# Gated delta net projections: queries and keys handed on before values, convolution taps read from PSUM, weights in blocks of one feature tile

## The chip, the cores and the metric

The kernel runs on one core of a Trainium2 chip. The metric is device time in microseconds (us) of one execution, lower is better. Before the change the median of 3 runs is 1668.59 us (1667.01 to 1671.13). The engines are named as the profile names them: PE (TensorE; PEld is its weight load), DVE (VectorE), ACT (ScalarE), POOL (GpSimd) and SP, whose queue issues the weight transfers.

## The reference

Two transformer blocks one after the other, in float32, on 272 tokens (16 meta tokens and 256 of the input) of width 1024; 48 rows of padding at the front are masked in the reference. The change is in one mixer only, the gated delta net of the first layer. Cut to that:

```python
proj = h @ w_in                        # 272 x 1024 @ 1024 x 6176
qkv = silu(causal_depthwise_conv(proj[..., :4096], conv_w))    # 4 taps per feature
z = proj[..., 4096:6144]               # output gate; two more groups give beta and g
q, k, v = split(qkv)                   # 8 heads of 128 for q and k, 16 for v
q, k = l2_normalize(q), l2_normalize(k)
# per chunk and head: A = I + tril(k k^T * beta * decay); solve A X = [v*beta, k*beta*exp(G)]
# scan over chunks: v_new = u - w S;  o = q S + attn v_new;  S = S*gt + k^T v_new
out = (rms_norm(o) * silu(z)) @ w_out
```

Everything else of the two blocks (residual additions, the feed-forward blocks, an mLSTM, three attention branches) is unchanged.

## The kernel before

Activations lie feature by feature: a tile holds 128 features on the partitions and 272 tokens along the free axis. A float32 product is made of three float32r matmuls, high by high, high by low and low by high. `wload` (L357) brings a block of weights of 512 KB from HBM into one of 3 `wraw` buffers; ACT rounds it to the high part `wh` (CAST), and POOL, in this stage, subtracts to get the low part `wl` in two halves. `linear_g` (L398) then accumulates, for one or two tiles of 128 output features, 24 matmuls of 272 columns per tile into the PSUM tiles `ps`, of which there are two, and calls a function on each finished tile.

In this stage that function is `conv4` (L974). ACT copies the PSUM tile to `cx` in SBUF and scales it by the last tap into `cy`; DVE adds the three other taps from `cx`; ACT takes a tanh (`cth`), and DVE or, for features from tile 14 on, POOL, makes the activated tile `kv`. `gdn_proj` (L991) does so for a group g of the four groups of heads: two tiles of keys, two of queries, four of values, each pair from blocks of 256 columns and 4 of the 8 input tiles, that is two blocks per pair.

A chain then follows for each group and each of two chunks c of 128 tokens. `before` (L1349) waits until all of `gdn_proj` is done. `unit_kq` (L1003) transposes queries and keys (`kqp`), sums squares on ACT, takes an inverse root in 11 small DVE operations (`rq_v`, `rq_y`, `rq_a`), scales (`kqtok`) and transposes back. `gdn_pre` (L1118) makes the decays (`dp`, ACT exponential `BA`), the products `kk`, and the token-major values (`vp`, `bv`). `gdn_core` (L1145) inverts the triangular matrix in doubling steps (`rtp` first, then `yp`, `Y`, `w` and the update of `RT` on DVE, at the end `zp`, `r2p`), applies it (`up`) and advances the state (`sp`, `op`); four lanes, each with its own PSUM bank, take the four groups one after the other. `after` (L1366) normalises and transposes back (`otp`). A short tail handles the last 16 tokens. `gdn_gates` (L899) makes beta and the decays' exponents from a narrow product `psba`: about twenty DVE operations on `lp`, `gg`, sums `gp` on PE, and `stk`, `rp`, `rw`.

The order on PE is written while the program is recorded. Each piece of work is a generator that yields what it will need; `Threads.run` (L153) takes the first live generator, in the list's order, whose inputs a small model of the engines holds to be ready. The chains stand ahead of the projections in that list, so the projections' matmuls (in steps of three) fill PE where no chain step counts as ready. PE then runs this order as written and waits at any instruction whose input is late. The order on DVE, ACT and POOL is made by the scheduler of the language below. The last piece of projection work is `gdn_z` (L1440), eight pairs of gate tiles; after it `project_out` starts with the matmuls `ps<-og`.

Of the kernel before, what the change touches and what calls it, by code (L numbers as in the profile page):

```python
# [21 lines left out]
T = S + NM  # L22
# [186 lines left out]
class Kern:  # L209
    def __init__(self, ctx, tc, ins, out):  # L210
        self.tc, self.nc, self.ctx = tc, tc.nc, ctx
        nc = tc.nc
        self.th = Threads()
        self.mem_done, self.half = Event(), Event()
        self.pause = [Event() for _ in range(3)]
        self.mwt = {}
        self.ready = {}
        self.V, self.A, self.PE, self.G = (self.th.engine(*e) for e in (
            ("V", nc.vector), ("A", nc.scalar), ("PE", nc.tensor), ("G", nc.gpsimd)))
        self.SY = nc.sync  # L220
        self.i = ins
        self.out = out

        self.const = self.pool(ctx, "const", 1)
        self.p_raw = self.pool(ctx, "praw", 3)
        self.p_hl = self.pool(ctx, "phl", 3)
        self.p_x = self.pool(ctx, "px", 8)
        self.p_h = self.pool(ctx, "ph", 14)
        self.p_s = self.pool(ctx, "psm", 2)
        self.p_t = self.pool(ctx, "ptiny", 2)  # L230
        self.lane = None
        self.ordered = False
        self.mixing = False
        self.near_load = self.seg = 0
        self.mid = None
        self.gctx = ExitStack()
        self.pp = self.pool(self.gctx, "pq", 2, space=PSUM)
        self.p_v = self.pool(self.gctx, "pkvg", 8)
        self.p_l = self.pool(self.gctx, "plane", 1)
        self.p_lp = self.pool(self.gctx, "planep", 1, space=PSUM)  # L240
# [37 lines left out]
        return t  # L278

    def ps(self, shape=(128, T), name="ps"):  # L280
        return self.pp.tile(list(shape), F32, tag="pp", name=name)

    def pcore(self, shape=(128, 4, 128), name="pcs"):
        return self.pc.tile(list(shape), F32, tag="pc", name=name)
# [533 lines left out]
    def embed(self):  # L818
# [15 lines left out]
        with self.tc.manual_schedule(engines={mybir.EngineType.DVE}):  # L834
# [21 lines left out]
            for t, (o, P) in enumerate(TT):  # L856
                self.ts(rd[:P, t, :P], self.ident[:P, :P], r[:P, t:t + 1], ALU.mult)
            self.columns(self.norms, 0)
            low = {1: prefetch(0, KD, 6144, 32), 3: prefetch(0, 4, 1024, 256), 6: prefetch(4, 4, 1024, 256)}
            self.masks()  # L860
            for k in range(KD):
                self.lane = k % 4
# [11 lines left out]
    def residual(self):  # L874

        for k in range(KD):
            yield [f"p{k % 4}", 10.0 + 1.0 * k]
            self.lane = k % 4
            p = self.plane("trx", (128, T))
            for t, (o, P) in enumerate(TT):  # L880
                self.tr(p[:, o:o + P], self.xt[t][k // 4][:P, (k % 4) * 128:(k % 4) * 128 + 128], P)
            self.A.copy(self.hs[k], p[:])
# [91 lines left out]
    def conv4(self, ps, ct, out):  # L974

        w = lambda j: self.pv(PV_GC + j * 32 + ct)
        y = self.sm(name="cy")
        x = self.p_l.tile([128, T], F32, tag="cx", name="cx", bufs=3)
        self.A.copy(x[:], ps)
        self.act(y[:], ps, AF.Copy, scale=w(3))  # L980
        for s in (1, 2, 3):
            self.stt(y[:, s:], x[:, :T - s], w(3 - s), y[:, s:], ALU.mult, ALU.add)
        th = self.sm(name="cth", tag="th")
        self.act(th[:], y[:], AF.Tanh, scale=0.5)
        if ct >= 14:
            self.tt(th[:], th[:], y[:], ALU.mult, self.G)
            self.tt(out, th[:], y[:], ALU.add, self.G)
        else:
            self.stt(out, th[:], 1.0, y[:], ALU.add, ALU.mult)

    def gdn_proj(self, X, g):  # L991
        W = self.i["gdn_w_in"][0]
        qs, ks, v0, v1 = (self.vslot() for _ in range(4))
        for base, dst in ((1024 + g * 256, ks), (g * 256, qs), (2048 + g * 512, v0), (2304 + g * 512, v1)):
            yield from self.linear_g(W, base, 256, KD, X, T, lambda m, p: self.conv4(p, base // 128 + m, dst[:, m, :]))
        tl = slice(256, T)
        self.G.tensor_copy(self.kqtail[:, 0, 2 * g:2 * g + 2, :], ks[:, :, tl])
        self.G.tensor_copy(self.kqtail[:, 1, 2 * g:2 * g + 2, :], qs[:, :, tl])
        for n, v in enumerate((v0, v1)):
            self.G.tensor_copy(self.vtail[:, 4 * g + 2 * n:4 * g + 2 * n + 2, :], v[:, :, tl])  # L1000
        return qs, ks, (v0, v1)

    def unit_kq(self, x, c):  # L1003


        n = len(x)
        yield list(x) + [f"pu{c}"]
        self.lane = f"u{c}"
        ss = self.tiny([128, n], "kqss")
        p = self.plane("kqp", (128, n, 128))  # L1010
        for h in range(n):
# [6 lines left out]
        kq = self.ring(f"kq{c}", "kqtok", (128, n, 128))  # L1018
        for h in range(n):
            self.act(kq[:, h, :], p[:, h, :], AF.Copy, scale=r[:, h:h + 1])  # L1020
        yield [kq[:], f"pu{c}", 0.8]
        self.lane = f"u{c}"
        p2 = self.plane("kqp2", (128, n, 128))
        for h in range(n):
            self.tr(p2[:, h, :], kq[:, h, :])
# [89 lines left out]
        self.tt(e[:], kk[:, :, None, :].to_broadcast([128, 2, 2, 128]), e[:], ALU.mult)  # L1115
        return e

    def gdn_pre(self, q, c, kqT, v):  # L1118


        sl = slice(c * 128, c * 128 + 128)
        h0 = 2 * q
# [9 lines left out]
                    self.mm(d[:, kind, h, :], selc(kind, h), rw, kind == 0 and h == 0, False)  # L1132

        BA = yield from self.decays(kqT[:, 0, :], kqT, diff, 0, self.nG[:, c, h0:h0 + 2])
        yield [BA[:], f"pu{c}"]
        self.lane = f"u{c}"
        vp = self.plane("vp")
        bv = self.ring(f"bv{c}", "bv")
# [1 line left out]
            self.tr(vp[:, h, :], v[:, h, sl])  # L1140
        for h in range(2):
            self.act(bv[:, h, :], vp[:, h, :], AF.Copy, scale=self.beta[:, c, h0 + h:h0 + h + 1])
        return BA, bv

    def gdn_core(self, q, c, kq, kqT, BA, bv, ss, state_of):  # L1145

        h0 = 2 * q
        lane = self.lane = (q % 2) * 2 + c
        R2 = yield from self.wy_inverse(BA[:, 0], 2, 128)
        aT = BA[:, 1]  # L1150
        S_ = self.St[q]
        if c:
# [163 lines left out]
    def gdn(self, X):  # L1316
# [7 lines left out]
        proj_done, after_done = events(), events()  # L1324
# [7 lines left out]
        def projections():  # L1332
            todo, nz = list(range(4)), 0
            while todo or nz < 8:
                if todo and (todo[0] < 2 or all(ev.on for ev in pre_done[todo[0] - 2])):
                    g = todo.pop(0)
                    self.lane = None
                    proj[g] = yield from self.gdn_proj(X, g)
                    proj_done[g].set()
                elif nz < 6 or not todo:  # L1340
                    if nz == 6:
# [5 lines left out]
                    yield from pre_done[todo[0] - 2]  # L1347

        def before(g, c):  # L1349
            yield proj_done[g]  # L1350
            qs, ks, vs = proj[g]
            for n in (c, 2 + c):
                if g > 1:
                    yield core_done[g - 2][n]
            u = yield from self.unit_kq([t[:, m, ch[c]] for m in range(2) for t in (ks, qs)], c)
            yield gates_done
            for m in range(2):
                j = 2 * g + m - 3
                if j >= 0:
                    yield core_done[j // 2][j % 2 * 2 + c]  # L1360
                kq, kqT = (t[:, 2 * m:2 * m + 2, :] for t in u)
                pre[g, 2 * m + c] = (kq, kqT) + (yield from self.gdn_pre(2 * g + m, c, kqT, vs[m]))
                pre_one[g][2 * m + c].set()
            pre_done[g][c].set()

        def after(g):  # L1366
# [7 lines left out]
        def first_chunks():  # L1374
            yield from self.gdn_gates(X)
            gates_done.set()
            for g in range(4):
                yield from before(g, 0)
                if g == 0:
# [46 lines left out]
                    split(len(Y) - 1, slice(0, 256))  # L1426
            gating_done.set()

        self.th.add([lane(n) for n in range(4)] + [first_chunks(), second_chunks(), gating()])
# [1018 lines left out]
```

## Time and profile before

| | |
|---|---|
| median of 3 runs | 1668.59 us |
| profiled execution | 1671.11 us, of which the span of the trace is 1669.3 us |
| mean granted TensorE clock | 0.973 of full speed |
| this stage, from the gates' product to the first `ps<-og` | 21.32 us to 368.32 us |

The stage is the first fifth of the span. The profile's page gives busy times over the whole span; for this stage the same numbers are taken from its own stretches, the order of waiting from the list of waits and the chain that ended last, and single steps from the timeline. In those views a bracket after an instruction is the time for which its engine stood idle before it, and the instruction that ended the idling. The rows stand below, in groups.

### The profile page before, as it was taken

The page shows a single profiled execution, that of the slowest core. Times are in us where ns is not written, and L with a number is a line of the kernel's source. Part 1 is how long each engine was busy: PE and PEld are TensorE (multiplying, and loading weights), DVE is VectorE, ACT ScalarE, POOL GpSimd, SP SyncE. Part 2 cuts the span into 40 slices and gives each one's busy share as a digit, 9 for nine tenths or more (in the row PEclk, how much of TensorE's full clock was granted, in tenths as well). Part 3 has the DMA queues.
Part 4 walks back from the last instruction along what each step waited for, and adds up shares of the span by engine and source line. Part 5 has one row for each costly group of instructions (what it writes and reads, how often), then busy time and mean ns, then how long its engine had stood idle before and what let it go on. Part 6 is the DMA issues. An engine that isn't in the chain of part 4 may idle for free.

```text
span 1669.3 us, 31255 instructions
## 1 busy us (share of the span) xinstructions
PE 1564.4 (94%) x11980; PEld 1475.4 (88%) x11980; DVE 1120.0 (67%) x2223; ACT 927.9 (56%) x1877; POOL 579.2 (35%) x535
## 2 busy tenths in 40 slices
PE   8889888899999998999899998999997899999999
PEld 6788778799899997888899998999985789999987
DVE  5788877766888757457877668464659663566643
ACT  4567767655566554446566556454553655564542
POOL 3574555320200002550344441122275548511221
PEclk9799999999999999999999999999998999999999
DMA  5331221226355554335366564566553335656564
GB/s 158 89 89 52 69 64 47 77 90 214 106 178 174 169 175 111 96 115 164 107 185 192 175 185 148 163 199 192 173 166 111 111 93 150 183 164 188 180 189 151
DMA packets 239100, 235.39 MB, mean 141 GB/s; under 512 B 11511, under 2 KB 226407, under 8 KB 238951
## 3 DMA queue, kind: packets, MB, share of 16 engines
q1 hardware_dynamic: 238326, 231.86, 46.4%
q8 instruction: 94, 1.54, 0.4%
q0 software_dynamic: 496, 1.41, 0.4%
q14 instruction: 56, 0.45, 0.1%
q10 hardware_dynamic: 128, 0.13, 0.0%
HBM read 232.32 MB, written 1.05 MB: 140 GB/s over the span
## 4 chain that ended last, share of the span: by engine, by line
PE 68%; DVE 22%; ACT 5%; DMA 3%; issue 2%; POOL 0%; ACTq 0%; POOLq 0%; DVEq 0%
PE ps L190 52%; PE pst L190 5%; DVE cy L190 3%; DVE rq_a L190 3%; ACT wh L190 2%; DVE RT L190 2%; DVE wl L190 1%; DVE rq_y L190 1%; PE memp L190 1%; DMA wraw<-in_ffn_w_up_dram 1%; DVE xn L190 1%; PE rsp L190 1%; DVE on L190 1%; PE w L190 1%; PE up L190 1%
## 5 line engine op out<-in xcount | busy, mean ns | idle before, releaser
L190 PE MATMUL ps<-xhl,wh 128*128 128x256 f32 (+2 forms) x4496 | 861.6, 294 | 28.9 <-DVE py L190 11.1
L190 PEld LDWEIGHTS ps<-xhl,wh 128*128 128x128 f32 x4496 | 703.0, 193 | 38.3 <-DVE py L190 6.9
L190 ACT CAST wh<-wraw 128x1024 fp32r<-128x1024 f32 (+2 forms) x436 | 448.0, 1029 | 389.8 <-PE ps L190 255.9
L190 PE MATMUL ps<-xhl,wl 128*128 128x256 f32 (+2 forms) x2248 | 626.0, 287 | 0.8 <-DVE wl L190 0.8
L383 POOL TENSOR_TENSOR wl<-wraw,wh 128x512 fp32r<-128x512 f32 (+3 forms) x264 | 334.7, 1291 | 658.2 <-ACT wh L190 622.8
L190 PEld LDWEIGHTS ps<-xhl,wl 128*128 128x128 f32 x2248 | 423.9, 192 | 1.0 <-DVE wl L190 1.0
L190 DVE TENSOR_TENSOR wl<-wraw,wh 128x1024 fp32r<-128x1024 f32 (+2 forms) x237 | 287.4, 1213 | 182.4 <-ACT wh L190 179.2
L190 POOL TENSOR_TENSOR wl<-wraw,wh 128x512 fp32r<-128x512 f32 x134 | 173.9, 1319 | 153.1 <-ACT wh L190 136.2
L190 PE MATMUL ps<-hh,wh 128*128 128x256 f32 (+1 forms) x1056 | 191.1, 283 | 0.0
L190 PEld LDWEIGHTS ps<-hh,wh 128*128 128x128 f32 x1056 | 163.2, 189 | 0.0
L190 PE MATMUL ps<-hh,wl 128*128 128x256 f32 (+1 forms) x528 | 149.7, 284 | 0.0
L190 DVE SCALAR_TENSOR_TENSOR fy<-ps,pvt,fy 128x256 f32<-128x256 f32 (+2 forms) x176 | 84.9, 488 | 25.1 <-ACT fy L190 23.2
L190 PEld LDWEIGHTS ps<-hh,wl 128*128 128x128 f32 x528 | 99.4, 188 | 0.0
L190 DVE SCALAR_TENSOR_TENSOR cy<-cx,pvt,cy 128x271 f32<-128x271 f32 (+2 forms) x96 | 74.5, 779 | 13.5 <-ACT cy L190 12.5
L190 DVE TENSOR_TENSOR hh<-fy,hh 128x256 fp32r<-128x256 f32 (+1 forms) x88 | 64.4, 735 | 13.2 <-ACT hh L190 12.8
L190 POOL MEMSET mvt<- 128x4 f32 x4 | 0.4, 102 | 176.0 <-PE ps L190 176.0
L190 ACT ACTIVATE fy<-ps,pvt 128x272 f32<-128x272 f32 (+1 forms) x88 | 49.5, 568 | 12.3 <-PE ps L190 11.8
L190 DVE TENSOR_TENSOR py<-ps,rstd 128x256 f32<-128x256 f32 x72 | 29.9, 420 | 37.9 <-PE ps L190 37.9
L190 PE MATMUL pst<-wh,hh 128*128 128x512 f32 x176 | 55.1, 394 | 0.0
L190 ACT CAST hh<-fy 128x256 fp32r<-128x256 f32 (+1 forms) x88 | 35.7, 407 | 29.8 <-DVE fy L190 29.0
L190 DVE CAST_PREDICATED RT<-lvl,w 128x512 f16<-128x512 uint8 x67 | 44.9, 683 | 7.1 <-PE w L190 6.8
L190 PE MATMUL ps<-og,wh 128*128 128x272 f32 x256 | 48.6, 289 | 0.1
(523 smaller groups left out, 2420.4 us busy)
## 6 DMA issues: line engine op xcount, KB each, us to landing
wraw<-in_ffn_w_up_dram SPq DMA_DIRECT2D x88, 512.0 KB
wraw<-in_ffn_w_gu_dram SPq DMA_DIRECT2D x88, 512.0 KB
wraw<-in_ffn_w_down_dram SPq DMA_DIRECT2D x79, 512.0 KB
wraw<-in_gdn_w_in_dram SPq DMA_DIRECT2D x48, 512.0 KB
wraw<-in_w_in_dram SPq DMA_DIRECT2D x41, 512.0 KB
wraw<-in_ml_w_in_dram SPq DMA_DIRECT2D x24, 512.0 KB
wraw<-in_gdn_w_out_dram SPq DMA_DIRECT2D x16, 512.0 KB
wraw<-in_ml_w_out_dram SPq DMA_DIRECT2D x8, 512.0 KB
```

The costliest lines, as they stand in the source:

```text
L190: r = f(*args, **kw)
L383: eng.tensor_tensor(l[:, a, b], r[:, a, b], h[:, a, b].bitcast(F32), ALU.subtract)
```

## The change

- `gdn_proj` projects one tile of 128 features at a time, from a block of 128 columns and all 8 input tiles (still 512 KB), and sets an event `kq_done` as soon as the two key and two query tiles are convolved. Before each tile it yields a key for the PSUM bank that the tile will reuse, so that the recording model sees when that bank comes free (`free`).
- `before` starts on `kq_done`. The values' part of `gdn_pre` is a generator of its own, `gdn_values`, which runs when the whole group is projected (for group 0 after both heads' matrices, else after each), and `gdn_core` waits for it only behind the inversion.
- `conv4` reads the three taps from the PSUM tile; the copy `cx` is gone.
- `gdn_gates` is a thread of its own, and the first chunk's `unit_kq` of group 0 uses bank `p0`.
- The transposes of the residual (`trx`) have later start marks.

```diff
     def ps(self, shape=(128, T), name="ps"):
-        return self.pp.tile(list(shape), F32, tag="pp", name=name)
+        t = self.pp.tile(list(shape), F32, tag="pp", name=name)
+        self.taken.append(t.tensor.name)
+        return t
+
+    def free(self, t):
+        n = self.taken.index(t.tensor.name)
+        key = f"pp{n % 2}"
+        self.th.bank[key] = self.taken[n - 2] if n > 1 else None
+        return key
...
-            low = {1: prefetch(0, KD, 6144, 32), 3: prefetch(0, 4, 1024, 256), 6: prefetch(4, 4, 1024, 256)}
+            low = {1: prefetch(0, KD, 6144, 32), 3: prefetch(0, KD, 1024, 128), 6: prefetch(0, KD, 1152, 128)}
...
-            yield [f"p{k % 4}", 10.0 + 1.0 * k]
+            yield [26.0 + 1.5 * k]
...
-        x = self.p_l.tile([128, T], F32, tag="cx", name="cx", bufs=3)
-        self.A.copy(x[:], ps)
         self.act(y[:], ps, AF.Copy, scale=w(3))
         for s in (1, 2, 3):
-            self.stt(y[:, s:], x[:, :T - s], w(3 - s), y[:, s:], ALU.mult, ALU.add)
+            self.stt(y[:, s:], ps[:, :T - s], w(3 - s), y[:, s:], ALU.mult, ALU.add)
...
-            yield from self.linear_g(W, base, 256, KD, X, T, lambda m, p: self.conv4(p, base // 128 + m, dst[:, m, :]))
+            for m in range(2):
+                ps = self.ps((128, T))
+                yield [self.free(ps)]
+                yield from self.linear_g(W, base + m * 128, 128, KD, X, T,
+                                         lambda _, p: self.conv4(p, base // 128 + m, dst[:, m, :]), [ps])
+            if dst is qs:
+                kq_done.set((qs, ks))
...
         R2 = yield from self.wy_inverse(BA[:, 0], 2, 128)
+        yield values
+        bv = values.v
...
-            yield proj_done[g]
-            qs, ks, vs = proj[g]
+            yield kq_done[g]
+            qs, ks = kq_done[g].v
...
-                pre[g, 2 * m + c] = (kq, kqT) + (yield from self.gdn_pre(2 * g + m, c, kqT, vs[m]))
+                BA = yield from self.gdn_pre(2 * g + m, c, kqT)
+                pre[g, 2 * m + c] = kq, kqT, BA, values[g, 2 * m + c]
                 pre_one[g][2 * m + c].set()
+                if g:
+                    yield proj_done[g]
+                    values[g, 2 * m + c].set((yield from self.gdn_values(2 * g + m, c, proj[g][2][m])))
+            if not g:
+                yield proj_done[g]
+                for m in range(2):
+                    values[g, 2 * m + c].set((yield from self.gdn_values(2 * g + m, c, proj[g][2][m])))
```

Three places show how instructions move. The first is PE at the transposes `kqp` of group 0. The numbers behind the names tell tiles apart: `kv_330` and `kv_329` are the group's keys and queries, `ps_698` is its last value tile, and in the program after the change `ps_649` is its first value tile. Before:

```order
L190 MATMUL ps_698<-xhl_142,wh_731 128x272 x2
L190 MATMUL ps_698<-xhl_142,wl_732 128x272
L190 MATMUL ps_698<-xhl_143,wh_731 128x272 x2
L190 MATMUL ps_698<-xhl_143,wl_732 128x272
L190 MATMUL kqp_801<-eye_106,kv_330 128x128
L190 MATMUL kqp_801<-eye_106,kv_329 128x128
```

After:

```order
L190 MATMUL ps_649<-xhl_136,wh_651 128x272 x2
L190 MATMUL ps_649<-xhl_136,wl_652 128x272
L190 MATMUL trx_660<-eye_106,xt_91 128x128
L190 MATMUL trx_660<-eye_106,xt_93 128x128
L190 MATMUL trx_660<-eye_106,xt_95 128x16
L190 MATMUL kqp_666<-eye_106,kv_330 128x128
L190 MATMUL kqp_666<-eye_106,kv_329 128x128
```

The transposes stand behind 192 of the stage's 1152 projection matmuls before and behind 123 after. Counted the same way, the first `rtp` stands behind 288 and then 198, and the last `otp` behind 1104 and then 1053.

The second place is DVE ahead of the first inverse root of group 0 (`rq_v`, which reads the sums of squares `kqss`). Before:

```order
L190 SCALAR_TENSOR_TENSOR cy_761<-cx_762,pvt_117,cy_761 128x271
L190 SCALAR_TENSOR_TENSOR cy_761<-cx_762,pvt_117,cy_761 128x270
L190 SCALAR_TENSOR_TENSOR cy_761<-cx_762,pvt_117,cy_761 128x269
L190 SCALAR_TENSOR_TENSOR cy_772<-cx_773,pvt_117,cy_772 128x271
L190 SCALAR_TENSOR_TENSOR cy_772<-cx_773,pvt_117,cy_772 128x270
L190 SCALAR_TENSOR_TENSOR cy_772<-cx_773,pvt_117,cy_772 128x269
L190 TENSOR_SCALAR rq_v_814<-kqss_800 128x4
```

After:

```order
L190 SCALAR_TENSOR_TENSOR kv_329<-cth_595,cy_590 128x272
L190 SCALAR_TENSOR_TENSOR cy_640<-ps_598,pvt_117,cy_640 128x271
L190 SCALAR_TENSOR_TENSOR cy_640<-ps_598,pvt_117,cy_640 128x270
L190 SCALAR_TENSOR_TENSOR cy_640<-ps_598,pvt_117,cy_640 128x269
L190 TENSOR_SCALAR rq_v_679<-kqss_665 128x4
```

Of the values' taps, six stand directly ahead of the root before (and six more ahead of those), and three after.

The third place is PE at the sums `gp` of the gates, which read `gg` from DVE. Before:

```order
L190 MATMUL trx_508<-eye_106,xt_90 128x128
L190 MATMUL trx_508<-eye_106,xt_92 128x128
L190 MATMUL trx_508<-eye_106,xt_94 128x16
L190 MATMUL ps_462<-xhl_142,wh_496 128x272 x2
L190 MATMUL ps_462<-xhl_142,wl_497 128x272
L190 MATMUL ps_462<-xhl_143,wh_496 128x272 x2
L190 MATMUL ps_462<-xhl_143,wl_497 128x272
L190 MATMUL gp_519<-gg_404,cc_89 128x16 x2
```

After:

```order
L190 MATMUL ps_425<-xhl_142,wh_230 128x272 x2
L190 MATMUL ps_425<-xhl_142,wl_231 128x272
L190 MATMUL ps_425<-xhl_143,wh_230 128x272 x2
L190 MATMUL ps_425<-xhl_143,wl_231 128x272
L190 MATMUL gp_459<-gg_403,cc_89 128x16 x2
```

`gp` stands behind 84 projection matmuls before and behind 48 after. From the first `ps<-og` on PE's rows are the same in both programs.

## Rows read from the trace of the kernel before

**Rows 1.** The page: span, and busy time with share of the span and instructions.

```profile
span 1669.3 us, 31255 instructions
PE 1564.4 (94%) x11980; PEld 1475.4 (88%) x11980; DVE 1120.0 (67%) x2223; ACT 927.9 (56%) x1877; POOL 579.2 (35%) x535
```

**Rows 2.** Stretches: length; busy PE, PEld, DVE, ACT, POOL; clock; DMA share; GB/s.

```profile
40.00:55.00 15.00, 10.58 (x45) 9.40 (x46) 10.04 (x32) 5.48 (x18) 5.00 (x5) 0.54 0.17 53
94.00:361.00 267.00, 233.16 (x2012) 212.95 (x2013) 211.88 (x517) 177.74 (x554) 139.54 (x157) 0.96 0.24 68
361.00:368.40 7.40, 6.89 (x54) 6.60 (x52) 3.53 (x13) 6.25 (x11) 0.00 (x0) 1.00 0.42 144
```

**Rows 3.** The chain that ended last, 94 to 361 us: shares by line.

```profile
by line: PE ps L190 18.3%; DVE RT L190 9.8%; DVE cy L190 9.5%; DVE rq_a L190 6.7%; DVE on L190 4.4%; PE w L190 4.1%; PE up L190 4.1%; PE dp L190 3.3%; PE yp L190 2.8%; issue 2.7%; DVE rq_y L190 2.5%; PE kk L190 2.5%; PE op L190 2.2%; DVE zs
```

**Rows 4.** PE's waits, 94 to 361 us: total, times, longest.

```profile
PE yp L190 <- DVE RT L190: 13.7, 10, 3.3
PE otp L190 <- DVE on L190: 5.0, 3, 4.4
```

**Rows 5.** PE's waits, 21 to 94 us.

```profile
PE gp L190 <- DVE gg L190: 5.2, 1, 5.2
PE ps L190 <- ACT cy L190: 1.4, 3, 1.0
```

**Rows 6.** The page and 20 to 362 us: busy us, mean ns | idle before.

```profile
L190 DVE SCALAR_TENSOR_TENSOR cy<-cx,pvt,cy 128x271 f32<-128x271 f32 (+2 forms) x96 | 74.5, 779 | 13.5 <-ACT cy L190 12.5
L190 ACT COPY cx<-ps 128x272 f32<-128x272 f32 x32 | 12.4, 389 | 2.8 <-PE ps L190 2.7
```

**Rows 7.** The taps alone, 94 to 361 us.

```profile
L190 DVE SCALAR_TENSOR_TENSOR cy<-cx,pvt,cy 128x271 f32<-128x271 f32 (+2 forms) x63 | 45.2, 720 | 5.2 <-ACT cy L190 4.7
```

**Rows 8.** By tile, whole span: duration min/median/max in ns, first and last start.

```profile
L190 DVE SCALAR_TENSOR_TENSOR cy<-cx,pvt,cy x96: 476/512/1583, 33.8 to 257.6; 128x271 f32<-128x271 f32 x32, 128x270 f32<-128x270 f32 x32, 128x269 f32<-128x269 f32 x32
L190 DVE SCALAR_TENSOR_TENSOR fy<-ps,pvt,fy x176: 468/486/501, 443.5 to 940.4; 128x256 f32<-128x256 f32 x88, 128x271 f32<-128x271 f32 x44, 128x270 f32<-128x270 f32 x44
L190 DVE TENSOR_TENSOR hh<-fy,hh x88: 409/432/1540, 453.1 to 1606.9; 128x256 fp32r<-128x256 f32 x66, 128x272 fp32r<-128x272 f32 x22
```

**Rows 9.** Timeline around the gates, 33 to 45 us: start, length, idle before.

```profile
33.79 0.77 DVE L190 SCALAR_TENSOR_TENSOR cy<-cx,pvt,cy 128x271 f32<-128x271 f32 x1
...
36.33 1.53 DVE L190 SCALAR_TENSOR_TENSOR cy<-cx,pvt,cy 128x269 f32<-128x269 f32 x1
...
39.41 1.54 DVE L190 SCALAR_TENSOR_TENSOR cy<-cx,pvt,cy 128x270 f32<-128x270 f32 x1
...
44.42 1.20 PE L190 MATMUL gp<-gg,cc 128*128 128x16 f32 x6 [5.21 <-DVE gg L190]
```

**Rows 10.** Timeline, 66 to 75 us.

```profile
66.34 1.04 PE L190 MATMUL kqp<-eye,kv 128*128 128x128 f32 x8
...
67.44 7.13 DVE L190 SCALAR_TENSOR_TENSOR cy<-cx,pvt,cy 128x271 f32<-128x271 f32 x6 [1.22 <-ACT cy L190]
...
68.51 0.51 ACT L190 ACTIVATE cy<-ps,pvt 128x272 f32<-128x272 f32 x1
68.89 0.30 ACT L190 ACTIVATE junk<-kqp 128x128 f32<-128x128 f32 x1
...
71.39 0.43 ACT L190 ACTIVATE cth<-cy 128x272 f32<-128x272 f32 x1 [1.85 <-DVE cy L190]
...
74.49 0.16 DVE L190 TENSOR_SCALAR rq_v<-kqss 128x4 f32<-128x4 f32 x1
```

**Rows 11.** The chain that ended last, 394 to 420 us: start, length.

```profile
394.43 24.19 PE ps L190 x192
```

**Rows 12.** Timeline at the stage's end.

```profile
360.88 0.38 PE L190 MATMUL otp<-eye,on 128*128 128x128 f32 x2
...
368.32 0.56 PE L190 MATMUL ps<-og,wh 128*128 128x272 f32 x2
```

More of the change, by code (lines that the diff above doesn't have):

```diff
@@ L231, in __init__ @@
         self.lane = None
+        self.taken = []
         self.ordered = False
@@ L989, in conv4, with gdn_proj @@
             self.stt(out, th[:], 1.0, y[:], ALU.add, ALU.mult)
[L991 removed]
+    def gdn_proj(self, X, g, kq_done):
         W = self.i["gdn_w_in"][0]
@@ L1001, in gdn_proj, with unit_kq @@
         return qs, ks, (v0, v1)
-    def unit_kq(self, x, c):
+    def unit_kq(self, x, c, lane=None):
         n = len(x)
-        yield list(x) + [f"pu{c}"]
-        self.lane = f"u{c}"
+        lane = f"u{c}" if lane is None else lane
+        yield list(x) + [f"p{lane}"]
+        self.lane = lane
         ss = self.tiny([128, n], "kqss")
@@ L1020, in unit_kq @@
             self.act(kq[:, h, :], p[:, h, :], AF.Copy, scale=r[:, h:h + 1])
-        yield [kq[:], f"pu{c}", 0.8]
-        self.lane = f"u{c}"
+        yield [kq[:], f"p{lane}", 0.8]
+        self.lane = lane
         p2 = self.plane("kqp2", (128, n, 128))
@@ L1116, in decays, with gdn_pre @@
         return e
-    def gdn_pre(self, q, c, kqT, v):
+    def gdn_pre(self, q, c, kqT):
         sl = slice(c * 128, c * 128 + 128)
@@ L1134, in gdn_pre, with gdn_values @@
         BA = yield from self.decays(kqT[:, 0, :], kqT, diff, 0, self.nG[:, c, h0:h0 + 2])
-        yield [BA[:], f"pu{c}"]
+        return BA
+    def gdn_values(self, q, c, v):
+        sl = slice(c * 128, c * 128 + 128)
+        h0 = 2 * q
+        yield [v[:], f"pu{c}"]
         self.lane = f"u{c}"
@@ L1142, in gdn_pre, with gdn_core @@
             self.act(bv[:, h, :], vp[:, h, :], AF.Copy, scale=self.beta[:, c, h0 + h:h0 + h + 1])
-        return BA, bv
-    def gdn_core(self, q, c, kq, kqT, BA, bv, ss, state_of):
+        return bv
+    def gdn_core(self, q, c, kq, kqT, BA, values, ss, state_of):
         h0 = 2 * q
@@ L1323, in gdn @@
         proj, state = {}, events(8)
-        proj_done, after_done = events(), events()
+        proj_done, after_done, kq_done = events(), events(), events()
+        values = {(g, n): Event() for g in range(4) for n in range(4)}
         pre, pre_one, core_done = {}, [events() for _ in range(4)], [events() for _ in range(4)]
@@ L1337, in projections @@
                     self.lane = None
-                    proj[g] = yield from self.gdn_proj(X, g)
+                    proj[g] = yield from self.gdn_proj(X, g, kq_done[g])
                     proj_done[g].set()
@@ L1354, in before @@
                     yield core_done[g - 2][n]
-            u = yield from self.unit_kq([t[:, m, ch[c]] for m in range(2) for t in (ks, qs)], c)
+            u = yield from self.unit_kq([t[:, m, ch[c]] for m in range(2) for t in (ks, qs)], c, None if g or c else 0)
             yield gates_done
@@ L1372, in after, with gates, first_chunks @@
             after_done[g].set()
-        def first_chunks():
+        def gates():
             yield from self.gdn_gates(X)
             gates_done.set()
+        def first_chunks():
             for g in range(4):
@@ L1427, in gating @@
             gating_done.set()
-        self.th.add([lane(n) for n in range(4)] + [first_chunks(), second_chunks(), gating()])
+        self.th.add([lane(n) for n in range(4)] + [gates(), first_chunks(), second_chunks(), gating()])
         self.columns(self.convs, PV_GC)
```

## The prediction

> **What bounds the kernel now.** I read the page first, then the stretches, then the chain that ended last with PE's waits, and the timeline at three places. Over the whole span PE is the busiest engine with 94% [rows 1], and the reader is to see in the stretches that this does not hold in the stage that changes: the chains' middle, 94 to 361 us, has PE busy for 233.2, DVE for 211.9 and ACT for 177.7 of 267 us [rows 2], and none is full. The chain of that stretch goes through PE's projection matmuls for 18.3%, DVE's update of `RT` for 9.8% and the convolution taps `cy` for 9.5% [rows 3]: several engines hand over to each other, and each hand-over queues behind filler. Where PE stands still there, it is mostly for DVE: 13.7 us for `RT`, 5.0 us for `on` [rows 4]. In the front it stands 5.2 us for the gates' `gg` and 1.4 us for a PSUM bank [rows 5]. [...]
>
> **What a moved matmul is worth.** The stage's PE work is the same before and after, so I add up its order first. A projection matmul in an unbroken run takes 24.19 / 192 = 0.126 us [rows 11]. The first `rtp` comes behind 90 fewer of them (288 to 198): -11.3 us. Between there and the last `otp` there were 1104 - 288 = 816 and are now 1053 - 198 = 855, 39 more: +4.9 us. Behind the last `otp`, where 48 took part of the 7.4 us up to `ps<-og` [rows 12], there are now 99, 51 more: +6.4 us. The three cancel. Starting the chains earlier therefore earns nothing in itself; it earns what PE stops losing in waits. The rest of the sum is about waits alone.
>
> **Taps from PSUM.** The 96 taps take 74.5 us, 0.78 each [rows 6], but 0.51 in the median, and up to 1.58 [rows 8]: they are stretched where POOL works. The feed-forward block has the same form with a PSUM operand, `fy<-ps,pvt,fy`: 0.47 to 0.50 us over 176 instructions, in stretches where its neighbour `hh<-fy,hh`, with both inputs in SBUF, reaches 1.54 [rows 8]. No row has it beside this stage's POOL work, so the price lies between 0.47 and the 0.78 of today; I take 0.49, by the nearest row, which has the same operands. At three places this is on the path.
> First, behind the transposes of group 0. They end at 67.4 us, and the root `rq_v` starts at 74.5, because six taps of 7.13 us stand ahead of it and because ACT's sums of squares (from 68.89 on) wait behind a tanh that itself waited for taps [rows 10]. Six taps at 0.49 would be 2.9; the new order has three there, but then the squares are next to be late, so I credit 7.1 - 2.9 = 4.2 us and no more: **-4.2**.
> Second, the gates. Three taps ahead of `gg` took 0.77, 1.53 and 1.54 [rows 9]; at 0.49 each `gg` is 2.4 us earlier. But `gp` now stands behind 48 matmuls instead of 84, PE is there 36 x 0.126 = 4.5 us earlier, and the wait of 5.2 becomes 5.2 + 4.5 - 2.4 = 7.3 us. What is queued behind it on PE is filler that the order sum has already counted as done; so the longer stop is a cost: **+2.1**. [...]
> Third, the middle. There 63 taps take 0.72 us each [rows 7], and the chain spends 9.5% of 267 = 25.4 us on them [rows 3]. At 0.49 that share shrinks by 0.32: **-8.1**. The bounds are 0, if what waited behind the taps then waits for something else, and the 14.5 us of busy time that 63 taps lose.
> [...]
>
> **The copy `cx`** goes: 32 x 0.389 = 12.4 us of ACT [rows 6]. I count it at nothing, since ACT is busy for 67% of the middle [rows 2] and the scaled copy `cy` that the taps wait for stays; at most it is worth the 20 or so copies of the middle, 7.8 us.
>
> **Bank held longer.** Today a bank is free when ACT has made `cx` and `cy`; afterwards only when the third tap is done. Between two uses of a bank PE does the other bank's 24 matmuls, 24 x 0.126 = 3.0 us at least. With free engines the bank is held for ACT's 0.51 [rows 10] and three taps, 2.0 us: no wait. In the middle 24 matmuls take 267 / 34 = 7.9 us, which leaves room. I take 0; the lower bound is 0 too (today's 1.4 us could at best go), the upper one is the third rival.
>
> **What else moves.** Weights: 32 blocks of 512 KB for these tiles before and after, with the same rounding on ACT and the same two halves on POOL, and as many issues on SP's queue; only the row of a block is shorter. With the DMA engines at 0.24 in the middle [rows 2] even twice the transfer time would stay hidden: 0, upper bound the wait for a late block, which the trace does not price. The values' part (`vp`, `bv`) leaves the way to `rtp`; it is needed only behind the inversion, and in the new PE order group 0's `vp` stand at 213 to 231 matmuls, the first `r2p` at 339, so the wait that `gdn_core` gains should end long before: 0. Were it late, the lane's `up` and all behind it on PE would stand. The later marks for `trx` move eight short transposes among the filler: 0.
>
> **Sum.** -4.2 + 2.1 - 8.1 = -10.2 us. The profiled execution took 1671.1 us, so 1660.9; it is 2.5 us above the median of the runs, so I forecast **1658 us** for the median.
>
> **Rivals.** (1) *DVE sets the pace.* If the middle is as long as DVE and ACT need, all the freed time counts: 14.5 of taps and 7.8 of copies, -4.2 + 2.1 - 22.3 = -24.4, 1644 us. For it: DVE at 79% with PE's longest waits on it [rows 2, 4]; against it: the largest share of the chain is PE's own filler [rows 3]. (2) *The freed time is off the path.* The tap's place in the chain is taken by PE or POOL, and other DVE operations with two SBUF inputs meet POOL instead: the middle gives 0, sum -2.1, 1666.5 us. If the taps stay stretched too, because `cy` still comes from SBUF, the change does not do what it says and only the gates' +2.1 is left, 1670.7 us. For it: a chain with shares this small and many [rows 3]. (3) *PE stands at the bank.* In the front ACT's `cy` of the second tile ended at 69.0 and its third tap at 74.6 [rows 10]: held for that, 5.6 us, a bank is 2.6 us late against the 3.0 us of the other bank. PE is in order, so chain steps stand behind it too. If DVE's line stays that long for the first eight tiles, it costs 8 x 2.6 = 20.8, and the front's -4.2 is gone: 2.1 - 8.1 + 20.8 = +14.8, 1683 us. It decides from the point where a tile's taps end more than 3.0 us behind its last matmul. Against it: the line was long because the taps were.
>
> **Chances.** Forecast 0.47, with a range of its own of 1652 to 1663; rival 1 0.17; rival 2 0.21; rival 3 0.15. The range 1642 to 1670 holds the forecast, most of rivals 1 and 2, and leaves out rival 3. A difference within 0.3%, 5 us, is what a measurement of this kernel can't tell from none, so faster means below 1663.6 and slower above 1673.6: faster is 0.43 of the forecast, all of rival 1 and 0.03 of rival 2, 0.63; slower is 0.12 of rival 3 and 0.01 of rival 2, 0.13; the same 0.24.
>
> **What would show it.** Taps `cy<-ps` at 0.47 to 0.50 us, with a maximum near the median; above 0.6 the third and first terms fall. `rq_v` within 4 us of the end of `kqp`. PE's wait at `gp` near 7 us; first `rtp` 11 to 15 us earlier than now. PE's waits for `ps` on DVE `cy` under 3 us in all; if they reach 15, rival 3. The first `ps<-og` near 358 us; near 344 means rival 1, near 366 rival 2. Behind it the two traces should run alike; a difference there would make the whole accounting wrong.

## The result, and the profile after

The changed kernel takes 1679.33 us in the median (1676.34 to 1682.86, 4 runs); the kernel before, run again beside it, 1667.81. The ratio is 1.0062, 95% interval 1.0044 to 1.008: slower by 0.6%, some 10 us, where 10 us faster was forecast. The forecast missed the sign and its range.

The page of the changed kernel, in the columns of [rows 1] and [rows 6]:

```profile
span 1677.6 us, 31196 instructions
PE 1566.2 (93%) x11980; PEld 1479.7 (88%) x11980; DVE 1095.7 (65%) x2223; ACT 920.2 (55%) x1845; POOL 573.6 (34%) x535
L190 DVE SCALAR_TENSOR_TENSOR cy<-ps,pvt,cy 128x271 f32<-128x271 f32 (+2 forms) x96 | 47.2, 491 | 10.7 <-ACT cy L190 9.6
```

The taps do what the change says: 0.491 us each, 47.2 us in all against 74.5. Their spread, by tile as in [rows 8]:

```profile
L190 DVE SCALAR_TENSOR_TENSOR cy<-ps,pvt,cy x96: 400/493/502, 30.3 to 273.0; 128x271 f32<-128x271 f32 x32, 128x270 f32<-128x270 f32 x32, 128x269 f32<-128x269 f32 x32
```

None is above 0.502 us, where the taps from the copy reached 1.58. The time is lost elsewhere. These rows of PE's timeline in the changed kernel (start, length, engine, operation, idle time before and what ended it) are the gates, the first `rtp`, the last `otp`, a stop at the stage's end and the first `ps<-og`:

```profile
38.25 1.20 PE L190 MATMUL gp<-gg,cc 128*128 128x16 f32 x6 [8.09 <-DVE gg L190]
...
78.06 0.27 PE L190 MATMUL rtp<-identh,RT 128*128 128x128 f16 x2
...
357.99 0.38 PE L190 MATMUL otp<-eye,on 128*128 128x128 f32 x2
...
368.01 0.52 PE L190 MATMUL ps<-xhl,wh 128*128 128x272 f32 x2 [2.38 <-DVE zs L190]
...
375.96 0.42 PE L190 MATMUL ps<-og,wh 128*128 128x272 f32 x2
```

The first `rtp` comes at 78.1 us, 16.3 earlier than before; the last `otp` at 358.0, only 2.9 earlier; the first `ps<-og` at 376.0, 7.6 later. So most of the lead is lost between the first `rtp` and the last `otp` (13.5 us), and 10.5 us more go behind the last `otp` (18.0 us up to `ps<-og`, 7.4 before [rows 12]). From `ps<-og` on, 1301.0 us of the span were left before and 1301.6 are now. What the stage's time is made of shows in its stretch up to `ps<-og`, first of the kernel before, then of the changed one (columns of [rows 2]):

```profile
21.00:368.30 347.30, 300.95 (x2448) 274.52 (x2449) 264.40 (x631) 221.36 (x664) 181.14 (x196) 0.93 0.26 74
```

```profile
21.00:376.00 355.00, 301.86 (x2447) 277.06 (x2446) 244.93 (x639) 218.01 (x641) 174.38 (x196) 0.92 0.26 72
```

PE works 301 and 302 us in both, at nearly the same granted clock (0.93 and 0.92). It stands 347.3 - 301.0 = 46.4 us before and 355.0 - 301.9 = 53.1 after. DVE and ACT have 19.5 and 3.4 us less to do, and PE waits 6.8 us more: 6.8 of the 7.7 us by which the stage is longer are what PE waits for. PE's waits of the changed kernel from 21 to 376 us (total, times, longest):

```profile
PE yp L190 <- DVE RT L190: 17.2, 6, 5.1
PE kqp L190 <- ACT kqtok L190: 8.6, 5, 3.9
PE ps L190 <- DVE zs L190: 8.2, 5, 2.9
PE gp L190 <- DVE gg L190: 8.1, 1, 8.1
PE kqp L190 <- DVE kv L190: 2.7, 3, 1.5
PE zp L190 <- DVE RT L190: 1.9, 1, 1.9
...
PE vp L190 <- POOL kv L190: 0.9, 1, 0.9
...
PE ps L190 <- DVE cy L190: 0.7, 2, 0.5
```

And of the kernel before, the same view:

```profile
PE yp L190 <- DVE RT L190: 13.7, 10, 3.3
PE kqp L190 <- ACT kqtok L190: 6.7, 4, 3.5
PE gp L190 <- DVE gg L190: 5.2, 1, 5.2
PE otp L190 <- DVE on L190: 5.0, 3, 4.4
PE zp L190 <- DVE RT L190: 4.8, 5, 2.2
PE ps L190 <- DVE zs L190: 2.6, 3, 1.9
PE rtp L190 <- DVE RT L190: 1.8, 1, 1.8
```

The waits for `RT` hardly fall (20.3 to 19.1) although DVE is rid of 27 us of taps. The waits for `otp` go (5.0 to under 1); those for `zs` (+5.6), for `kv` (+3.6), at the gates (+2.9) and for `kqtok` (+1.9) take more. The chain of waits from 94 to 361 us says the same, beside [rows 3]:

```profile
by line: PE ps L190 24.9%; DVE RT L190 7.4%; DVE rq_a L190 5.9%; PE w L190 5.7%; DVE on L190 5.3%; issue 3.9%; PE dp L190 3.8%; PE up L190 3.6%; PE yp L190 3.3%; DVE cy L190 3.1%; ACT junk L190 2.7%; PE ksp L190 2.3%; PE op L190 2.2%; ACT w
```

The taps' share falls from 9.5 to 3.1%, 17 us of 267, and that of PE's filler rises from 18.3 to 24.9%, 17.6 us. The shares always make up the whole chain, so this says what took the taps' place in it and not why.

### The profile page after: what moved, and what is told of

The parts are those of the page before. It is cut to its first block, busy times and chain, and to the rows that moved or that the text cites. A ratio compares the mean times of both kernels' runs of the same rounds, so it can differ in the third digit from the quotient of the medians.

```text
span 1677.6 us, 31196 instructions
## 1 busy us (share of the span) xinstructions
PE 1566.2 (93%) x11980; PEld 1479.7 (88%) x11980; DVE 1095.7 (65%) x2223; ACT 920.2 (55%) x1845; POOL 573.6 (34%) x535
## 4 chain that ended last, share of the span: by engine, by line
PE 72%; DVE 18%; ACT 5%; DMA 2%; issue 2%; POOL 0%; ACTq 0%; POOLq 0%; DVEq 0%
PE ps L190 56%; PE pst L190 5%; DVE rq_a L190 3%; ACT wh L190 2%; DVE rq_y L190 1%; DVE wl L190 1%; DVE RT L190 1%; PE w L190 1%; PE memp L190 1%; DVE on L190 1%; DMA wraw<-in_mem_w_kv_dram 1%; PE rsp L190 1%; DVE xn L190 1%; PE dp L190 1%; DVE cy L190 1%
## 5 line engine op out<-in xcount | busy, mean ns | idle before, releaser
L190 POOL TENSOR_TENSOR wl<-wraw,wh 128x512 fp32r<-128x512 f32 x134 | 169.8, 1289 | 173.4 <-ACT wh L190 160.0
L190 DVE TENSOR_TENSOR hh<-fy,hh 128x256 fp32r<-128x256 f32 (+1 forms) x88 | 64.4, 735 | 13.9 <-ACT hh L190 13.7
L190 DVE CAST_PREDICATED RT<-lvl,w 128x512 f16<-128x512 uint8 x67 | 45.4, 684 | 14.6 <-PE w L190 13.8
L190 DVE SCALAR_TENSOR_TENSOR cy<-ps,pvt,cy 128x271 f32<-128x271 f32 (+2 forms) x96 | 47.2, 491 | 10.7 <-ACT cy L190 9.6
L190 ACT ACTIVATE Y<-yp 128x256 f16<-128x256 f32 x99 | 37.1, 385 | 24.6 <-PE yp L190 24.0
```

The lines of the kernel that those rows point to most:

```text
L190: r = f(*args, **kw)
```

## The experiments

Ratios are to the kernel before, timed beside each run; its median moved between 1668.4 and 1671.9 us from one job to the next, so experiments are compared by ratio (0.1% is 1.7 us). "Replayed" means that the list of which thread advanced at each step of one kernel is written into another, so that PE's instructions keep their order; DVE, ACT and POOL are still laid out by the scheduler:

```diff
...
-            e = best[1]
-            self.clk["PE"] = max(self.clk["PE"], best[0])
+        for c in PICKS:
+            e = self.live[int(c, 16)]
...
```

**Taps and order apart.** e1 is the kernel before with the taps' lines of the change alone, replayed; e2 is the changed kernel with the copy `cx` back, replayed:

```diff
+        x = self.p_l.tile([128, T], F32, tag="cx", name="cx", bufs=3)
+        self.A.copy(x[:], ps)
...
-            self.stt(y[:, s:], ps[:, :T - s], w(3 - s), y[:, s:], ALU.mult, ALU.add)
+            self.stt(y[:, s:], x[:, :T - s], w(3 - s), y[:, s:], ALU.mult, ALU.add)
```

> The kernel before with the taps reading PSUM and without the copy cx, and with the steps of all threads replayed in the order of the kernel before, so that PE's instructions stand exactly as there. Theory A (the shorter taps are worth something on the path, and what made the change slower is the new order of the steps): 1656 to 1662 us, the two tap terms of the prediction, with PE waiting 5 to 10 us less between 94 and 361 us. Rival B (the taps' time is off the path; what waited behind a tap then waits for another DVE operation): 1665 to 1669, PE's waits in the middle within 3 us of 36. Rival C (the bank held through the third tap costs): above 1672, with PE waiting for DVE's cy.

Measured: 1672.84 us, ratio 1.002 (1.0007 to 1.0034). The waits for `RT` fell from 20.3 to 12.9, as theory A has it, but PE's waits for a bank that the taps still hold (rival C) went to 21 us. From 21 to 385 us:

```profile
PE ps L190 <- DVE cy L190: 21.0, 12, 5.0
PE yp L190 <- DVE RT L190: 7.5, 8, 1.6
...
PE zp L190 <- DVE RT L190: 4.5, 4, 2.3
...
PE rtp L190 <- DVE RT L190: 0.9, 1, 0.9
```

So rival C's wait eats what theory A's saves: PE stands 49.4 us in this stage against 46.4 before. The stage still ends 0.9 us earlier, at 367.4; in this trace the loss lies behind it (see the table below).

> The changed kernel with the copy cx put back and the taps reading it, steps replayed in the order of the changed kernel: PE's order is that of the changed kernel, only the taps' source differs. Theory A: 8 to 12 us slower than the changed kernel, 1687 to 1691. Rival B: 1677 to 1682, as the changed kernel. Rival C: faster than the changed kernel, below 1675.

Measured: 1694.45, ratio 1.0151 (1.0132 to 1.0171). In the changed order the taps from PSUM are worth 1.0151 - 1.0062 = 0.89%, 15 us, a little above theory A. The order, with the old taps, costs 25 us, and it does so in waits: PE stands 370.0 - 305.0 = 65.0 us, against 46.4 before and 53.1 in the changed kernel (columns of [rows 2]):

```profile
21.00:391.00 370.00, 304.95 (x2448) 277.66 (x2449) 269.45 (x642) 225.41 (x673) 180.93 (x196) 0.92 0.25 70
```

This is why the taps' gain is not to be seen in the result.

**The two halves.** e3 has the early begin with the old blocks of 256 columns and the old taps; e5 has the narrow blocks, the yielded bank and the taps from PSUM, with the begin of before.

> The first half of the change alone: chains begin when queries and keys are convolved, values later, gates as a thread of their own, late residual transposes; with blocks of 256 columns and the taps from the copy as before. Theory A (the order costs): 1678 to 1690. Rival B (the early start costs nothing and the narrow blocks or the bank are at fault): 1664 to 1670.

Measured: 1693.02, ratio 1.0142 (1.0123 to 1.016), 24 us slower, a little beyond theory A's range. With e2 it shows that the order of the early begin costs this with either width of block. The gates' thread and the marks of `trx` are part of that order: e3's waits hold one stop of 9.0 us at `trx`, e2's hold none.

> The second half of the change alone, on the kernel before: blocks of 128 columns, a bank yielded as free before each tile, taps from PSUM; chains still begin when the whole group is projected. Theory D (in the order of the kernel before the taps are worth their two terms once no matmul stands at a bank that the taps still hold; e1 lost 21 us of PE's time there): 1656 to 1662 us, PE's waits for DVE's cy under 5 us. Rival E (in that order PE waits for something else instead): 1666 to 1671, the waits for RT and on as in the kernel before.

Measured: 1671.88, ratio 1.0011 (1.0002 to 1.0021). Rival E: this half gives nothing. It changes the blocks and with them PE's order as well as the taps, so what the taps alone give in it is not shown. The bank costs 2.9 us only, `RT` 15.4 instead of 20.3, but the gates' wait is 7.7, `kqtok` 8.7 and `on` 6.3, 5.8 us more together than before. So the halves do not add up: 24 and 2 us apart, 10 together.

**Narrow blocks.** e8 is the changed kernel with `linear_g(W, base, 256, ...)` again, two tiles beside each other.

> The changed kernel with blocks of 256 columns as before (two tiles beside each other, no bank yielded as free), everything else as in the changed kernel. If narrow blocks with the yielded bank are what keeps the taps' hold of a bank off PE: 10 us or more slower than the changed kernel, above 1688, with PE waiting for DVE's cy as in e1 (21 us there). If they only move instructions: 1674 to 1684.

Measured: 1686.36, ratio 1.0101 (1.0087 to 1.0114); the size came out at 6.5 us, less than expected. The order is planned anew and has one stop of 8.0 us at `trx`, so the size is not that of the bank alone. From 21 to 390 us:

```profile
PE ps L190 <- DVE cy L190: 22.8, 12, 3.0
```

The third rival of the forecast, PE standing at the bank, is a real mechanism: 21 to 23 us in e1 and e8. The narrow blocks and the yielded bank keep it off (0.7 us in the changed kernel).

**Which early begin costs.** In `before(g, c)`, e6 lets only group 0 begin early, e7 only groups 1 to 3:

```diff
-            yield kq_done[g]
+            yield proj_done[g] if g else kq_done[g]     # e6
+            yield kq_done[g] if g else proj_done[g]     # e7
```

> The changed kernel, with the early begin for group 0 only: groups 1 to 3 wait until their values are projected too. Theory F (the early begin of groups 1 to 3 is what costs: their transposes stand right behind the convolution of their queries, and PE stands for kv, kqtok and RT): 1655 to 1668 us, with the first rtp still at 78 and no wait for DVE's kv at kqp behind 100 us. Rival G (the early begin of group 0 costs by itself, since its steps then meet fewer filler matmuls later): 1677 to 1690.

Measured: 1671.26, ratio 1.0006 (0.999 to 1.0023), above theory F's range of times, but 9 us below the changed kernel, with the first `rtp` at 78 as there and no wait at `kqp` for DVE's `kv`.

> The mirror image: group 0 begins when its values are projected too, groups 1 to 3 begin early as in the changed kernel. Theory F: 1676 to 1690 us, first rtp near 90 and PE waiting at kqp of group 1. Rival G: 1660 to 1670.

Measured: 1679.15, ratio 1.0056 (1.0043 to 1.0069). Theory F holds: the early begin of groups 1 to 3 carries the whole loss, and that of group 0 shows none. The stage of e6, in the same columns, ends 12.7 us earlier than that of the changed kernel, with PE standing 46.0 us instead of 53.1:

```profile
21.00:363.28 342.28, 296.27 (x2447) 271.38 (x2445) 233.75 (x629) 214.87 (x633) 175.54 (x196) 0.95 0.27 76
```

**Values between the decays.** e4 moves the values of every group behind the decays of both head pairs, as group 0 has them.

> The changed kernel with one move: in every group, as now in group 0 only, the values' transposes come behind the decays of both head pairs, so that lanes 2 and 3 don't stand behind the last value projection of their group. If that thread order is what made lanes 2 and 3 of group 3 start only 6 us earlier (rtp at 279 and 281 us against 285 and 288 before, where lanes 0 and 1 gained 16): rtp of these lanes at 272 or earlier and 1670 to 1675 us. If the lanes are held by something else: 1677 to 1682.

Measured: 1689.18, ratio 1.0112 (1.0093 to 1.0132), slower than the changed kernel. That idea fell: the four `rtp` of group 3 came at 271, 274, 277 and 291 instead of 263, 266, 279 and 281. The move also planned the rest anew, so it proves nothing on the values by themselves.

**What stands in PE's way.** The longest wait of the changed kernel's middle is at 225 us. Its timeline there, DVE and POOL with PE's wait:

```profile
219.31 0.67 DVE L190 TENSOR_SCALAR on<-on,rq_o 128x128 f32<-128x128 f32 x2
...
219.90 0.20 DVE L190 CAST RT<-w 32x64 f16<-32x64 f32 x1
220.03 3.71 DVE L190 TENSOR_SCALAR on<-on,rq_o 128x128 f32<-128x128 f32 x6
220.78 2.48 POOL L190 TENSOR_TENSOR wl<-wraw,wh 128x512 fp32r<-128x512 f32 x2 [0.19 <-ACT wh L190]
223.66 0.68 DVE L190 CAST_PREDICATED RT<-lvl,w 128x512 f16<-128x512 uint8 x1
224.26 0.49 DVE L190 SCALAR_TENSOR_TENSOR cy<-ps,pvt,cy 128x271 f32<-128x271 f32 x1
224.78 0.22 DVE L190 CAST RT<-w 32x64 f16<-32x64 f32 x1
225.06 0.37 PE L190 MATMUL yp<-RT,Br 128*128 128x128 f16 x2 [5.12 <-DVE RT L190]
```

Eight scalings `on` of a finished group stand ahead of the `RT` of a running one, and six of them take 3.71 us while POOL makes `wl`. The next longest waits for `RT` look different. At 183 us roots of a group that has just begun, beside POOL's `wl`, and a tap stand ahead of `RT`:

```profile
179.89 2.49 POOL L190 TENSOR_TENSOR wl<-wraw,wh 128x512 fp32r<-128x512 f32 x2 [5.22 <-ACT wh L190]
179.95 1.23 DVE L190 SCALAR_TENSOR_TENSOR rq_a<-rq_y 128x4 f32<-128x4 f32 x1
181.10 0.48 DVE L190 SCALAR_TENSOR_TENSOR cy<-ps,pvt,cy 128x271 f32<-128x271 f32 x1
181.51 0.88 DVE L190 TENSOR_TENSOR rq_a<-rq_a,rq_v 128x4 f32<-128x4 f32 x1
182.43 0.22 DVE L190 CAST RT<-w 32x64 f16<-32x64 f32 x1
...
182.71 0.39 PE L190 MATMUL yp<-RT,Br 128*128 128x128 f16 x2 [3.68 <-DVE RT L190]
```

e9 moves the scalings to ACT, replayed; e10 moves POOL's `wl` of the input projection to DVE, replayed:

```diff
-            self.ts(on[:, h, :], on[:, h, :], r[:, h:h + 1], ALU.mult)
+            self.act(on[:, h, :], on[:, h, :], AF.Copy, scale=r[:, h:h + 1])   # e9
```

> The changed kernel with its steps replayed, so that PE's order is kept; only the 32 scalings of on by the root move from DVE to ACT. Theory H (in the new order PE's waits for RT, 19 us, come from DVE doing six to eight on of a finished group in a row, stretched by POOL, ahead of the RT of a group begun early: 3.7 us of on ahead of the wait of 5.1 us at 225): PE's waits for RT at 12 us or less and 1668 to 1674 us. Rival I (RT would be late anyway behind taps and roots): RT waits of 16 to 20 us, 1677 to 1682.

Measured: 1672.12, ratio 1.0009 (0.9998 to 1.002), 0.5% or 9 us below the changed kernel with PE's order kept. Theory H's time; the waits for `RT` fell less than it said, at `yp` from 17.2 to 13.5 and in all from 19.1 to 14.0: the one at 225 us is 3.1 instead of 5.1, the one at 183 us stays at 3.7.

> The changed kernel with its steps replayed; the low parts wl of the input projection's 48 blocks are made on DVE (1.22 us a block) instead of on POOL (two halves of 1.29). Theory J (POOL's wl is what stretches DVE's operations with SBUF inputs): rq_a<-rq_a,rq_v at 0.17 us in the mean against 0.35, on at 0.35 against 0.54, none above 0.9 except beside POOL's kv and cth. DVE carries 48 x 1.22 = 59 us more, so the time says little: 1670 to 1700. If the stretch has another cause, the means stay.

Measured: 1674.12, ratio 1.0027 (1.0012 to 1.0041). The two DVE groups from 21 to 376 us (busy us, mean ns | idle before), first in the changed kernel, then in e10:

```profile
L190 DVE TENSOR_SCALAR on<-on,rq_o 128x128 f32<-128x128 f32 x32 | 15.3, 539 | 0.1
L190 DVE TENSOR_TENSOR rq_a<-rq_a,rq_v 128x4 f32<-128x4 f32 (+2 forms) x39 | 13.5, 353 | 0.5
```

```profile
L190 DVE TENSOR_TENSOR rq_a<-rq_a,rq_v 128x4 f32<-128x4 f32 (+2 forms) x39 | 7.6, 201 | 0.6
L190 DVE TENSOR_SCALAR on<-on,rq_o 128x128 f32<-128x128 f32 x32 | 7.4, 292 | 0.1
```

Theory J: without POOL's `wl` the same operations take about half, and the kernel is 0.35% faster than the changed one though DVE makes 51 blocks of `wl` for 63.2 us. In e10 `on` takes at most 0.67 us, and POOL is busy for 44.5 of the 267 us from 94 to 361, where it was 128.6. In the changed kernel `on` and `rq_a` are stretched (to 1.33 and 1.30 us), the taps with a PSUM operand (at most 0.502 us) are not: the one at 66.68 us took 0.48 beside POOL's `wl`. Why the ones are stretched and the others are not, no run shows.

**A version that beats both.** e11 is e6 with the scalings of `on` on ACT, planned anew; e15 the same, replayed in e6's order; e16 is e5 with them, replayed in e5's order; e12 is the kernel before with them, planned anew.

> Early begin for group 0 only (e6), with the scalings of on on ACT, order planned anew. If PE's waits for on and RT (13 us in e6) are worth something on the path: 1660 to 1667 us. If the end of the stage (ACT's two table loads and the last splits og, which e6 exposed) takes it back: 1668 to 1674.

Measured: 1659.72, ratio 0.9942 (0.9924 to 0.996): 0.6% faster than before and 1.2% than the changed kernel. Up to its `ps<-og` PE stands 333.9 - 293.2 = 40.7 us:

```profile
21.00:354.87 333.87, 293.17 (x2448) 268.78 (x2449) 227.56 (x609) 226.78 (x673) 175.07 (x196) 0.95 0.28 78
```

> e6 (group 0 early, 1671.3 us) with its steps replayed and on moved to ACT. If the move itself gives e11's gain: 1659 to 1663. If the gain is that of the order planned anew: 1667 to 1671.

Measured: 1662.94, ratio 0.995 (0.9931 to 0.9968): the move of `on` itself gives 0.56% on e6, most of e11's 0.64%.

e15 also says what the bursts of `on` are not. With `on` on ACT in both, the early begin of groups 1 to 3 still costs 1.0009 - 0.995 = 0.59% (e9 against e15), 10 us; with `on` on DVE it costs 1.0062 - 1.0006 = 0.56%, 9 us. So moving `on` is worth 9 us in either order, and `on` is not why the early begin costs. What the early begin adds in either case is PE's wait for `RT`; from 21 to 376 us, in e9, then in e15 (e6 has the same line as e15, the changed kernel 17.2):

```profile
PE yp L190 <- DVE RT L190: 13.5, 5, 3.7
```

```profile
PE yp L190 <- DVE RT L190: 7.3, 6, 2.1
```

> e5 (blocks and taps alone, every chain begins when its group is wholly projected, 1671.9 us) with its steps replayed and the scalings of on moved to ACT. If the early begin of group 0 earns nothing in itself: 1660 to 1665, as e15. If it is worth the 4 to 9 us by which e6's chains end sooner: 1666 to 1671.

Measured: 1666.63, ratio 0.998 (0.9965 to 0.9995), at the lower edge of the second guess; in this order the move of `on` gives 0.31%, 5 us. e15 and e16 differ by 0.3%, 5 us, with intervals that just touch: the early begin of group 0 is probably worth a few us once DVE is clear.

> The kernel before with the scalings of on on ACT and nothing else, order planned anew. If DVE's bursts of on are worth as much in the order of before: 1660 to 1666 us, with PE's waits for on (5.0 us) gone. If the order of before has them off the path: 1666 to 1671.

Measured: 1677.26, ratio 1.0039 (1.0017 to 1.006); both guesses missed. The waits for `on` fell to 2.1 us, but `yp` waited 17.3 us for `RT` instead of 13.7. The order was planned anew, and no replay was run, so how much of it is the order stays open. In its trace only 2.3 of the 8.5 us lie in the stage.

> e11 (group 0 early, on on ACT, 1659.7 us) with its steps replayed, the copy cx put back and the taps reading it. If the taps are worth something wherever DVE stands on PE's way: 8 to 15 us slower, 1668 to 1675, with longer waits of PE for RT. If their worth hangs on the early begin of groups 1 to 3, as the runs so far would also allow: 1658 to 1663.

Measured: 1682.48, ratio 1.0061 (1.0042 to 1.0081): in e11's order the taps from PSUM are worth 1.2%, 20 us, with groups 1 to 3 beginning late. So their worth is not tied to the early begin.

> e11 with the low parts wl of the input projection on DVE instead of POOL, order planned anew. If POOL's stretching of roots and RT costs more on the path than DVE's 59 us more of work: 1650 to 1657. If DVE's extra work eats it: 1659 to 1668.

Measured: 1675.72, ratio 1.0021 (1.0008 to 1.0034), slower than both guesses. DVE makes 50 blocks of `wl` and stands 39.5 us ahead of them for ACT's `wh`; in the changed kernel's order (e10) that was 29.4. These stops can at most explain why the stage is longer than e11's: it ends at 367.3, 1.0 us earlier than before, and what makes the kernel slower than before lies, in this trace, behind it.

**In the stage and behind it.** Behind the first `ps<-og` PE's order is the same in all these kernels. From each run's one trace, in us:

| run | first `ps<-og` | PE busy, from 21 us | PE stands | granted clock | rest of the span |
|---|---|---|---|---|---|
| before | 368.3 | 301.0 | 46.4 | 0.93 | 1301.0 |
| changed | 376.0 | 301.8 | 53.1 | 0.92 | 1301.6 |
| e1 | 367.4 | 297.0 | 49.4 | 0.96 | 1303.9 |
| e2 | 391.0 | 305.0 | 65.0 | 0.92 | 1301.7 |
| e5 | 368.3 | 298.5 | 48.8 | 0.93 | 1300.6 |
| e6 | 363.3 | 296.3 | 46.0 | 0.95 | 1306.9 |
| e9 | 365.8 | 297.8 | 47.0 | 0.94 | 1305.2 |
| e10 | 368.4 | 293.8 | 53.6 | 0.96 | 1299.1 |
| e11 | 354.9 | 293.2 | 40.7 | 0.95 | 1304.6 |
| e12 | 370.6 | 301.1 | 48.5 | 0.95 | 1307.2 |
| e14 | 367.3 | 297.9 | 48.4 | 0.95 | 1307.2 |
| e15 | 358.2 | 294.3 | 42.9 | 0.95 | 1303.0 |

Two things in it are not PE's waits. The same matmuls keep PE busy for 293 to 305 us: of the 13.5 us by which e11's stage is shorter than before, 7.8 are this and 5.7 are waits, and e10, whose stage has PE standing as long as the changed kernel's, is shorter by this alone. The granted clock goes with it in part only (e12 has 0.95 and 301.1). And the rest of the span differs by up to 8.1 us, as much as most effects here: e6 ends its stage 5.0 us earlier than before and is no faster. The granted clock differs there too. In e6, behind a stop of 2.4 us, it was 0.93 from the first `ps<-og` to 410 us, and in e6, e9, e12 and e14 0.96 from 1310 to 1350 us; before, it was 1.00 in both stretches. Whether an edit causes what lies behind the stage is not shown; the ratios contain it.

## Why the prediction was wrong

The step that failed is the first: "The three cancel. Starting the chains earlier therefore earns nothing in itself." It priced the order by counting matmuls, as if PE's waits did not depend on it. With the taps unchanged the new order costs 24 to 25 us (e2, e3), and PE's standing time rises from 46.4 to 65.0 us (e2). In the changed kernel the part of the order that costs is the early begin of groups 1 to 3: 9 us against e6, 10 with `on` on ACT (e9 against e15). What it adds is PE's wait for `RT` at `yp`, 17.2 us instead of 7.3. Starting the groups earlier puts their steps among those of the group before, and their roots share DVE's queue with its `RT`; PE, in order, stands behind whichever is late. That the roots are what delays `RT` is read from the timeline; no run moved them, and in e10, where POOL's `wl` no longer stretches them and DVE makes it instead, the wait is still 14.6 us. The bursts of `on` are not the reason, though moving them gets 9 of the 10 us back, since the move is worth as much without the early begin (e15).

Point by point:

- **Taps, price and sum.** 0.49 us was taken and 0.491 came. A tap from PSUM was no slower than one from the copy in SBUF, 0.493 us in the median against 0.512 [rows 8], and putting the copy back costs 15 us in e2 and 20 in e13. The two terms, -4.2 and -8.1, are -12.3; in the changed order the taps are worth -15 (e2), in e11's -20 (e13). In the order of before they are worth nothing (e1, 3 us slower), and PE stands at the bank. The sum is near the first of these by luck: the forecast read the taps' worth from the chain of the order that was given up, and there other waits took their place, as the second rival said.
- **First `rq_v`.** It starts at 58.8 us, 1.5 us behind the end of `kqp`, as said. But PE still waits 3.9 us for the second chunk's `kqtok`, a wait that was 3.5 us before and that the forecast's account of the front left out. Some of the root's small operations stand beside POOL's `wl`: one of 128x4 elements at 62.18 took 1.29 us.
- **Gates.** The stop is 8.1 us against 7.3 forecast: near.
- **First `rtp`.** 16.3 us earlier, 11 to 15 forecast. The last `otp` should have been 16.6 earlier (-11.3 + 4.9 - 4.2 + 2.1 - 8.1) and was 2.9. So the forecast broke in the middle: from the first `rtp` to the last `otp` it had 4.9 - 8.1 = -3.2 us, and +13.5 came. Of PE's waits for `RT` there it read the 13.7 us at `yp` alone; with `zp` and `rtp` they were 20.3.
- **Behind the last `otp`.** 51 matmuls more were forecast at +6.4 us; it was +10.5. The rest is mostly two stops of 2.38 and 1.56 us at a bank of `z`, whose `zs` stands behind the splits `og` on DVE, the first time beside POOL's `wl`, the second behind a `wl` of DVE's own. Before, there were 0.5 us of this at the end.
- **Bank.** 0 was taken and 0.7 us came. Without the narrow blocks it would have been the third rival (e8).
- **Weights, values, `trx`, copy.** The narrow blocks with the taps, without the early begin, cost 0.1% (e5), and PE's waits of the changed kernel name no late block. The values' waits are 0.9 us at `vp` and 0.3 at `bv`. The marks of `trx` were not tried alone.
- **Behind the stage.** The traces of these two kernels run alike, 1301.0 and 1301.6 us; those of the experiments differ by up to 8.1.

None of the rivals named what happened. The chance of 0.13 for slower stood almost wholly on the bank.

Open: which work on DVE delays `RT` when groups 1 to 3 begin early; which groups carry the 24 to 25 us that the order costs with the old taps; and why e5 gains nothing. For e5 the waits show four places that share it, but no replay divides taps and blocks there; e16 took `on` away and gained 0.3%.

## What to carry to other kernels

When a change lets work begin earlier on an in-order engine, count not only the instructions ahead of it but also the queues it will now share with the work it catches up: here DVE's. Price the order and the operations apart, by replaying one kernel's order in the other; the saving of an operation is only worth what the order lets it be (nothing, 15 and 20 us for the same 27 us of DVE time). A fix that wins the time back need not point at the cause: moving 32 small scalings to an engine with room was worth 9 us in the changed order, and as much in the order without the early begin, and 5 us in e5's; where the kernel before was planned anew with it (e12), 0.4% was lost. So try the fix in both orders.

## What the runs showed of the hardware

- DVE operations of 128x4 elements, 0.16 us in the median of the changed kernel, took up to 1.3 us there beside a POOL `tensor_tensor` of 1.28 us; without POOL's `wl` the mean of `rq_a` fell from 353 to 201 ns. The forecast saw this for the taps and did not apply it to the roots and scalings.
- On ACT a scaling of 128x128 took 0.39 us at any time (385 to 410 ns in e9), on DVE 0.27 to 1.33 in the changed kernel: the engine that is slower alone was the steadier one.
